# One more pair of K tiles by seven products in the first feed-forward of an encoder block

## The chip, the cores and the metric

The kernel runs on one core of a Trainium2 chip. The metric is the time of one execution in microseconds (us), device time, median of the runs. The whole block runs as one program; nothing is computed on the host but the arrangement of weights and inputs in memory.

## What is computed

One layer of an encoder on 256 tokens of width 2048: a feed-forward at half weight, a mixing stage with two recurrent branches, a cross-attention to 256 memory tokens, a second feed-forward, a last norm. The change lies in the first feed-forward alone:

```python
def rms_norm(x, g):
    y = x * rsqrt(mean(x * x, axis=-1, keepdims=True) + EPS)
    return y * g

def swiglu(h, w_up, w_down):                       # w_up 2048 x 11264, w_down 5632 x 2048
    gate, up = split(h @ w_up, 2, axis=-1)
    return (silu(gate) * up) @ w_down

x = x + 0.5 * swiglu(rms_norm(x, ffn1_norm), ffn1_w_up, ffn1_w_down)
...                                                # mixing, cross-attention
x = x + 0.5 * swiglu(rms_norm(x, ffn2_norm), ffn2_w_up, ffn2_w_down)
```

All inputs and weights are fp32.

## The kernel before

**Precision.** Matmuls run on the type fp32r. Each operand is split in a high part (a copy on ScalarE into fp32r, L138) and a low part (raw less high, on VectorE, L139), both by the helper `split`. A product a b is then three matmuls: high by high, low by high and high by low (function `three`: L547, L548 and, later, L550).

**Tiling of the first feed-forward.** The 5632 hidden features go in eleven groups of 512, numbered 0 to 10. In a group the 2048 input features are eight pairs of K tiles of 128, here called p0 to p7 (the digit is the pair's index, not its place in the order). The weights of a pair and a group are one tile `raw` of 128x2048, 1 MB: four blocks of 512 columns, up and gate for each of the two K tiles. x is the stationary side, 128x128, and there are two token tiles; so a pair is a 2x2 by 2x2 block product: token tiles by K tiles by (up, gate).

- A *plain* pair does it with eight products of 128x128 by 128x512, 24 matmuls. A *mixed* pair also has eight, written so that its results fall into the accumulators of the seven-product scheme; it needs differences of x ("less") as well. Both split the raw tile as a whole.
- A *fast* pair does it with seven products, 21 matmuls. It needs sums of the weights' blocks, four blocks `td`, made on VectorE (L285, L287, L288: `td` or, elsewhere, a raw buffer), and sums of x. It splits three raw blocks (128x1536, giving h and l) and the four blocks of sums in two halves of 128x1024 (giving th and tl). The halves of th are called th1 and th2 here.
- A fast pair that *adds* (p3, p4, p5, p6 from group 4 on) makes l of the raw blocks without VectorE: ScalarE writes the negated high part (L293), and a transfer from GpSimd's queue adds the raw weights to it in memory (L294).

**Down products.** A group's hidden features are multiplied by w_down in tiles of 128x2048 too, four such tiles after each group from group 3 on, called d1 to d4 here; one of four is made with the adding transfer (L254, L255, L263), the others are plain (split as a whole). The hidden features are turned by TensorE (L588) in between.

**Order.** `ffn_order` writes the order of pairs and down tiles by hand. `weights` prepares two tiles ahead of the one in use (three where a tile's low part is added by transfer). Within that, a scheduler in the layer below fixes the order of instructions of every engine when the program is built; at run time each engine works its queue in that order. Buffers are rings: raw 3, h 3 (h and th of a pair take two), l 3, wide 3 (td, tl and the evicted accumulators), slots 22 (operands of x, hidden operands, workspace). A load on SyncE's queue goes when its ring's buffer is free.

**Before the change**, from group 4 on the order is p1, p3, p4, p0, p2, p5, p6, p7, and p0 is mixed, the others fast. In group 3, p0 and p6 are mixed and made with the adding transfer.

**Sums of x.** `operand_pairs` makes for each pair of K tiles the split operand, the differences (`less`) and, in its inner function `sums`, the sums. For even pairs the differences would lie in the place of the sums, so the pairs in `BOTH` keep them in a tile of their own, `xd`, and get sums as well; these are made later, at places 16, 17 and 26 of the plan (`late_sums`).

Of the kernel before, what the change touches and what calls it, by code (L numbers as in the profile page):

```python
# [8 lines left out]
F32 = mybir.dt.float32  # L9
F32R = mybir.dt.float32r  # L10
ACT = mybir.ActivationFunctionType
ALU = mybir.AluOpType

P = 128
# [24 lines left out]
PAD = 16  # L39


def ffn_order(every=False):

    out = [(("mixed" if p > 5 else "fast") if every else "plain", 0, p) for p in range(8)]
    down = [("down", 0, 1, c, 0) for c in range(4)]  # L50
    for g in range(1, NG):
        if every:
            out += [("fast", g, p) for p in (1, 3, 4, 0, 2, 5, 6, 7)]
        elif g < 3:
            out += [(("mixed", "fast")[p % 2], g, p) for p in (0, 1, 2, 3, 5, 4, 7, 6)]
        else:
            out += [("mixed" if p == 0 or g == 3 and p == 6 else "fast", g, p)
                    for p in ((1, 3, 0, 4, 2, 6, 5, 7) if g == 3 else (1, 3, 4, 0, 2, 5, 6, 7))]
        if g > 2 and g % 2:
            down = [("down", g - 2, 2, c, b) for c in range(4) for b in (g - 2, g - 1)]  # L60
        n = 2 if g < 3 else 4
        out, down = out + down[:n], down[n:]
    return out + [("down", NG - 2, 2, c, b) for c in range(4) for b in (NG - 2, NG - 1)]


def adds(name, e):

    return name == "ffn1" and e[0] == "fast" and e[1] > 3 and e[2] in (3, 4, 5, 6)


def sums_ready(name, e):

    made = () if e[1] < 3 else (0, 5, 7) if e[1] % 2 else (0, 3, 5, 7)
    return name == "ffn2" and e[0] == "fast" and e[2] not in made
# [3 lines left out]
def block_kernel(ctx: ExitStack, tc: tile.TileContext, xT, xin, memT, vec, gfin, bgate, lruw, wu1, wd1, win, wv,  # L78
                 wg, wab, wout, wq, wk, wvm, wo, wu2, wd2, out_):
    nc = tc.nc  # L80
    pe, dve, act, sp = nc.tensor, nc.vector, nc.scalar, nc.sync
# [23 lines left out]
    def slot(dt=F32, name="slot"):  # L105
        return slots.tile([P, 1024], dt, name=name, tag="slot")
# [24 lines left out]
    x = [xt[k // 4][:, (k % 4) * T:(k % 4 + 1) * T] for k in range(KT)]  # L131
    ident = col("ident", 0, P)

    done = {}


    def split(h, l, raw):
        done["high"] = act.activation(h, raw, ACT.Copy).ins  # L138
        done["low"] = dve.tensor_tensor(out=l, in0=raw, in1=h.bitcast(F32), op=ALU.subtract).ins  # L139
# [4 lines left out]

    plan, ahead, made_ahead = [], [], []
    orders = {"ffn1": ffn_order(), "ffn2": ffn_order(every=True)}

    def plan_ffn(name, wu, wd):
        for e in orders[name]:
            src = wd[e[4], e[3]] if e[0] == "down" else wu[e[1], e[2]]  # L150
            kind = "fast" if e[0] == "fast" else "added" if e[:2] == ("mixed", 3) else "plain"
            if e[0] == "down" and 0 < e[4] < NG - 1 and e[4] % 2 == 0 and e[3] % 2:
                kind = "added"
            if adds(name, e):
                kind = "fast added"
            if sums_ready(name, e):
                kind = "ready"
                t = kept.tile([P, 2048], F32, name=f"t{e[1]}_{e[2]}")
                made_ahead.append((src, t))
                src = src, t  # L160
            plan.append(((name,) + e, src, kind))
# [4 lines left out]
    def plan_rows(name, w, g):  # L166
        plan.extend(((name, g, kq), w[g, kq], "plain") for kq in range(w.shape[1]))

    plan_ffn("ffn1", wu1, wd1)
    first_middle = len(plan)  # L170
    for hf in range(2):
# [12 lines left out]
    for name, w in (("mv", wvm), ("o", wo)):  # L184
        for g in range(4):
            plan_rows(name, w, g)
    first_second = len(plan)
    plan_ffn("ffn2", wu2, wd2)

    head, rest = [], {}  # L190
# [297 lines left out]

    BOTH = [2, 4, 6]
    xd = []

    def operand_pairs(src, gain, q, xg, out, every=False):


        for a in src:
# [8 lines left out]
            if every:  # L506
                less = None
                if q == 3:
                    if not i:
                        xd.append(slot(F32R, "xd"))  # L510
                    less = [xd[-1][:, a:a + 256] for a in (512 * i, 512 * i + 256)]
            elif 2 * q + i in BOTH:
                n = 512 * (BOTH.index(2 * q + i) % 2)
                if not n:
# [4 lines left out]
        def sums(which=((0, "less"), (0, "sums"), (1, "less"), (1, "sums"))):  # L519
            s = slot(name="xs")  # L520
            for i, ((h, l), less) in enumerate(out):
                a = [xg[:, i * 512 + j * P:][:, :P] for j in range(4)]

                def made(h, l, n, at, terms):
                    o = [s[:, at + j * P:][:, :P] for j in range(n)]
                    for j, (x, y, op) in enumerate(terms(o)):
                        dve.tensor_tensor(out=o[j], in0=x, in1=y, op=op)
                    split(h, l, s[:, at:at + n * P])

                if less and (i, "less") in which:  # L530
                    made(*less, 2, 0, lambda o: ((a[0], a[1], ALU.subtract), (a[2], a[3], ALU.subtract)))
                if (every or i or 2 * q in BOTH) and (i, "sums") in which:
                    if not every and not i and len(which) > 1:
# [31 lines left out]
    def ffn(name, pairs, sq, then, begin=(), sums=()):  # L565
# [38 lines left out]
        for at, e in enumerate(order):  # L604
# [3 lines left out]
            if kind != "down":  # L608
# [3 lines left out]
                for i, (a, b, n) in enumerate(PRODUCTS["ready" if sums_ready(name, e) else kind]):  # L612
                    u = uses[g, n]
                    if u[0] == (p, i):
                        accs[n] = bank()
                    own, less = pairs[p]
                    products.append((accs[n], part(own, a, P) if a >= 0 else part(less, -1 - a, P), part(w[b // 4] if fast else w, b % 4, 512),
                                     u[0] == (p, i), u[-1] == (p, i)))
                three(products, 3 if adds(name, e) else 0, adds(name, e) and p == 6)
                last = at + 1 == len(order) or order[at + 1][1] != g or following == "down"  # L620
                ends = kind != "plain" and uses[g, 0][-1][0] == p
# [51 lines left out]
    pairs1, sq1 = [], TokenSquares()  # L673
# [30 lines left out]
    def late_sums(q):  # L704
        with tc.issue_after(done["low"]):
            sums1[q](((0, "sums"),))

    for q, i in ((1, 16), (2, 17), (3, 26)):
        rest[i] = lambda q=q: late_sums(q)


    par = const.tile([P, 96], F32, name="par")
# [56 lines left out]
    xs = xs2.tiles  # L769
# [372 lines left out]
    for g in range(4):  # L1142
# [4 lines left out]
        for t in range(2):  # L1147
            s = slot(F32R, "vs")
            f = scoped["tmp2"].tile([P, 512], F32, name="vf", tag="part")
# [7 lines left out]
    for h in range(HEADS):  # L1157
        for j in range(4):
            acc = bank()
            for t in range(2):  # L1160
                ps = probs[h][:, t * 512:(t + 1) * 512]
                s = vs[h, t]
# [153 lines left out]
```

## Time and profile before

| what | us |
|---|---|
| median of 3 runs | 2426.14 |
| lowest and highest | 2425.5 and 2426.68 |
| span of the profiled execution | 2425.5 |
| first feed-forward in it, to the turn of the last group's hidden features | 648.0 |
| one of the groups 4 to 9 in it | 61.7 to 61.8 |
| group 10, between the same marks | 63.6 |

How it is read: the profile names engines PE (TensorE matmuls), PEld (its weight loads), DVE (VectorE), ACT (ScalarE), POOL (GpSimd), SP (SyncE); a letter q marks an engine's queue issuing a transfer. An instruction is named by its line in the kernel, then output <- inputs. In a row of the timeline the first number is the start in us from the start of the span, the second the time to the end of the last of xN merged instructions, and brackets give the idle time of the engine before it and what ended it. Matmuls overlap in their records, so their spacing is read from starts. The clock granted to TensorE is 0.998 of full speed over the span, so it plays no part. The lines themselves are shown in the prediction.

### The profile page before, as it was taken

How to read it: one execution, taken by the hardware profiler on the slowest of the kernel's cores; microseconds unless marked ns; L12 is line 12 of the kernel's file. 1: busy time of each engine (PE TensorE's matmuls, PEld its weight loads, DVE VectorE, ACT ScalarE, POOL GpSimd, SP SyncE). 2: the span in 40 equal slices, each digit the busy share in tenths (PEclk: the TensorE clock that was granted, in tenths of full speed). 3: DMA queues.
4: the chain of work that ended last, by engine and by line, in shares of the span. 5: the costliest groups of instructions: out<-in, count | busy, mean ns of one | idle time of the engine just before them, and what ended most of it. 6: DMA issues, size and time to landing. Idle time of an engine off the chain costs nothing.

```text
span 2425.5 us, 30763 instructions
## 1 busy us (share of the span) xinstructions
PE 2409.3 (99%) x12139; PEld 2013.6 (83%) x12139; DVE 2025.6 (84%) x2260; ACT 1455.0 (60%) x1485; POOL 102.2 (4%) x166
## 2 busy tenths in 40 slices
PE   9999999999999999999999999999999999999998
PEld 8888888888788888888888888888888788888887
DVE  7999999998876868779776788777789999999995
ACT  8567677777664454476434555445676666666664
POOL 0000000000000000000000000000000000000000
PEclk9999999999999999999999999999999999999999
DMA  7579999988858776778989889977798878787873
GB/s 294 195 229 287 272 272 270 275 269 268 266 183 323 268 289 241 294 289 323 346 313 349 310 332 354 335 272 263 264 343 308 285 266 293 273 286 276 294 273 144
DMA packets 102385, 684.31 MB, mean 282 GB/s; under 512 B 11361, under 2 KB 11617, under 8 KB 29281
## 3 DMA queue, kind: packets, MB, share of 16 engines
q1 hardware_dynamic: 78192, 518.68, 57.5%
q0 software_dynamic: 23328, 162.54, 22.4%
q8 instruction: 95, 1.56, 0.2%
q10 hardware_dynamic: 720, 1.13, 0.1%
q14 instruction: 50, 0.40, 0.0%
HBM read 619.39 MB, written 62.91 MB: 281 GB/s over the span
## 4 chain that ended last, share of the span: by engine, by line
PE 91%; DVE 3%; DMA 3%; ACT 1%; issue 1%; ACTq 0%; DVEq 0%; SPq 0%
PE acc L547 16%; PE acc L548 16%; PE acc L550 16%; PE acc L313 11%; PE acc L338 8%; PE acc L341 8%; PE acc L339 8%; PE acc L316 6%; DMA raw<-wd 2%; DVE tl L139 1%; ACT h L138 1%; DVE l L139 1%; PE acc L588 1%; PE acc L477 1%; DMA t<-prep 0%
## 5 line engine op out<-in xcount | busy, mean ns | idle before, releaser
L138 ACT ACTIVATE h<-raw 128x2048 fp32r<-128x2048 f32 (+3 forms) x578 | 870.5, 1531 | 620.2 <-PE acc L339 189.6
L139 DVE TENSOR_TENSOR l<-raw,h 128x2048 fp32r<-128x2048 f32 (+2 forms) x406 | 837.3, 2065 | 187.6 <-ACT h L138 186.1
L547 PE MATMUL acc<-h,xh 128*128 128x512 f32 x1241 | 485.2, 392 | 2.7 <-ACT h L138 2.4
L548 PE MATMUL acc<-h,xl 128*128 128x512 f32 x1241 | 483.0, 390 | 0.0
L338 PE MATMUL acc<-h,ops 128*128 128x512 f32 x832 | 326.8, 393 | 0.0
L339 PE MATMUL acc<-h,ops 128*128 128x512 f32 x832 | 324.5, 390 | 0.0
L547 PEld LDWEIGHTS acc<-h,xh 128*128 128x128 f32 x1241 | 233.3, 188 | 56.2 <-ACT h L138 8.0
L547 PE MATMUL acc<-h,hidop 128*128 128x512 f32 x704 | 276.5, 393 | 2.3 <-ACT h L138 2.2
L313 PE MATMUL acc<-ops,h 128*128 128x512 f32 x1152 | 278.2, 393 | 0.0
L548 PE MATMUL acc<-h,hidop 128*128 128x512 f32 x704 | 274.8, 390 | 0.0
L548 PEld LDWEIGHTS acc<-h,xl 128*128 128x128 f32 x1241 | 233.3, 188 | 47.5
L313 PEld LDWEIGHTS acc<-ops,h 128*128 128x128 f32 x1152 | 211.7, 188 | 41.6
L139 DVE TENSOR_TENSOR tl<-raw,h 128x1024 fp32r<-128x1024 f32 x172 | 203.7, 1220 | 14.9 <-ACT h L138 14.5
L341 PE MATMUL acc<-l,ops 128*128 128x512 f32 x832 | 205.8, 389 | 0.0
L550 PE MATMUL acc<-l,hidop 128*128 128x512 f32 x704 | 189.3, 389 | 0.0
L138 ACT ACTIVATE h<-td 128x1024 fp32r<-128x1024 f32 x126 | 131.3, 1057 | 92.9 <-PE acc L548 42.3
L341 PEld LDWEIGHTS acc<-l,ops 128*128 128x128 f32 x832 | 156.2, 188 | 32.4
L338 PEld LDWEIGHTS acc<-h,ops 128*128 128x128 f32 x832 | 156.2, 188 | 32.2
L339 PEld LDWEIGHTS acc<-h,ops 128*128 128x128 f32 x832 | 156.3, 188 | 31.5
L139 DVE TENSOR_TENSOR tl<-td,h 128x1024 fp32r<-128x1024 f32 x126 | 152.0, 1220 | 31.2 <-ACT h L138 31.0
L200 DVE TENSOR_TENSOR prep<-prep 128x512 f32<-128x512 f32 x232 | 159.7, 689 | 20.9 <-DMA prep<-wu 17.1
L550 PE MATMUL acc<-l,xh 128*128 128x512 f32 x645 | 176.4, 389 | 0.0
(242 smaller groups left out, 2739.4 us busy)
## 6 DMA issues: line engine op xcount, KB each, us to landing
raw<-wu SPq DMA_DIRECT2D x114, 1024.0 KB, 6.3
raw<-wd SPq DMA_DIRECT2D x88, 1024.0 KB, 6.3
prep<-wu POOLq DMA_DIRECT2D x58, 1024.0 KB, 7.8
t<-prep POOLq DMA_DIRECT2D x58, 1024.0 KB, 7.8
raw<-t SPq DMA_DIRECT2D x58, 1024.0 KB, 6.9
raw<-wu SPq DMA_DIRECT2D x58, 768.0 KB, 5.0
raw<-win SPq DMA_DIRECT2D x40, 1024.0 KB, 4.8
raw<-wg SPq DMA_DIRECT2D x32, 1024.0 KB, 6.1
```

The costliest lines, as they stand in the source:

```text
L138: done["high"] = act.activation(h, raw, ACT.Copy).ins
L139: done["low"] = dve.tensor_tensor(out=l, in0=raw, in1=h.bitcast(F32), op=ALU.subtract).ins
L200: dve.tensor_tensor(out=b[o], in0=b[x], in1=b[y], op=ALU.subtract)
L313: pe.matmul(acc, h[:, k * P:(k + 1) * P], xs[k], start=k == 0, stop=False)
L316: done["product"] = pe.matmul(acc[:, :T], l[:, k * P:(k + 1) * P], xs[k][:, :T], start=False, stop=k == KT - 1).ins
L338: pe.matmul(accs[t], x[:, t * P:][:, :P], h[j], start=first and j == 0, stop=False)
L339: pe.matmul(accs[t], x[:, T + t * P:][:, :P], h[j], start=False, stop=False)
L341: done["product"] = pe.matmul(accs[t], x[:, t * P:][:, :P], l[j], start=False, stop=last and j == 3).ins
L477: pe.transpose(acc[:, z * T + t * P:][:, :P], tile[:, t * 512 + (2 * y + z) * P:][:, :P], ident)
L547: pe.matmul(acc, ah, bh, start=start, stop=False)
L548: pe.matmul(acc, al, bh, start=False, stop=False)
L550: pe.matmul(acc, ah, bl, start=False, stop=stop)
```

## The change

From group 4 on, p0 is a fast pair too, and it is third in the order instead of fourth: p1, p3, p0, p4, p2, p5, p6, p7. The pairs that add stay the same four. p0 is added to `BOTH`, so its differences, which the mixed product of the groups 1 to 3 reads, go to `xd`, and its sums take the place after the first 512 columns. These sums are made by a new function `first_sums` at place 33 of the plan, which is in group 3, from the high and low parts of x added together. The orders of the groups 0 to 3 are only written in another way (the table `FIRST`: p plain, m mixed, M mixed with the adding transfer, f fast, a fast with the adding transfer).

```diff
+FIRST = [
+    "p0 p1 p2 p3 p4 p5 p6 p7",
+    "m0 f1 m2 f3 f5 m4 f7 m6",
+    "m0 f1 m2 f3 f5 m4 f7 m6",
+    "f1 f3 M0 f4 f2 M6 f5 f7",
+    "f1 a3 f0 a4 f2 a5 a6 f7",
...
+]
+KINDS = {"p": "plain", "m": "mixed", "M": "mixed", "f": "fast", "a": "fast"}
+
+def first(g):
+    return [(KINDS[e[0]], g, int(e[1])) for e in FIRST[g].split()]
 
 def ffn_order(every=False):
-    out = [(("mixed" if p > 5 else "fast") if every else "plain", 0, p) for p in range(8)]
+    out = [("mixed" if p > 5 else "fast", 0, p) for p in range(8)] if every else first(0)
...
-        elif g < 3:
-            out += [(("mixed", "fast")[p % 2], g, p) for p in (0, 1, 2, 3, 5, 4, 7, 6)]
         else:
-            out += [("mixed" if p == 0 or g == 3 and p == 6 else "fast", g, p)
-                    for p in ((1, 3, 0, 4, 2, 6, 5, 7) if g == 3 else (1, 3, 4, 0, 2, 5, 6, 7))]
+            out += first(g)
...
-    return name == "ffn1" and e[0] == "fast" and e[1] > 3 and e[2] in (3, 4, 5, 6)
+    return name == "ffn1" and e[0] == "fast" and f"a{e[2]}" in FIRST[e[1]]
...
-    BOTH = [2, 4, 6]
+    BOTH = [0, 2, 4, 6]
...
+    def first_sums():
+        (h, l), _ = pairs1[0]
+        s = slot(name="xs")
+        a, o = ([s[:, n + j * P:][:, :P] for j in range(4)] for n in (0, 512))
+        with tc.issue_after(done["low"]):
+            dve.tensor_tensor(out=s[:, :512], in0=h[:, :512].bitcast(F32), in1=l[:, :512].bitcast(F32), op=ALU.add)
+            for j, (x, y, op) in enumerate(((a[1], a[3], ALU.add), (o[0], a[0], ALU.subtract),
+                                            (a[1], a[0], ALU.subtract), (a[2], o[1], ALU.subtract))):
+                dve.tensor_tensor(out=o[j], in0=x, in1=y, op=op)
+            split(h[:, 512:], l[:, 512:], s[:, 512:])
+
+    rest[33] = first_sums
```

In the built program the order of SyncE's and GpSimd's transfers is unchanged but for the order of p0's and p4's tiles; on TensorE, VectorE and ScalarE the order changes from group 3 to the end of the first feed-forward and nowhere after it.

More of the change, by code (lines that the diff above doesn't have):

```diff
@@ L150, in plan_ffn @@
             src = wd[e[4], e[3]] if e[0] == "down" else wu[e[1], e[2]]
-            kind = "fast" if e[0] == "fast" else "added" if e[:2] == ("mixed", 3) else "plain"
+            kind = "fast" if e[0] == "fast" else "added" if name == "ffn1" and e[0] == "mixed" and f"M{e[2]}" in FIRST[e[1]] else "plain"
             if e[0] == "down" and 0 < e[4] < NG - 1 and e[4] % 2 == 0 and e[3] % 2:
```

6 rows, old and new, of the table FIRST are left out of this document.

## The prediction

> **What bounds the kernel now.** I read the page first, then windows of the first feed-forward group by group, then the order of work on each engine inside one group.
>
> ```profile
> PE 2409.3 (99%) x12139; PEld 2013.6 (83%) x12139; DVE 2025.6 (84%) x2260; ACT 1455.0 (60%) x1485; POOL 102.2 (4%) x166
> ```
>
> TensorE is busy 99% of the span, which says "TensorE bound" as a mean. The change touches seven groups, 4 to 10 of the eleven numbered 0 to 10, so these are read by themselves. The windows below run from one set of L588 transposes to the next; columns are length, busy time of PE, PEld, DVE, ACT and POOL, granted clock, DMA share, GB/s.
>
> ```profile
> 275.50:337.30 61.80, 61.66 (x276) 50.84 (x275) 56.41 (x57) 44.05 (x37) 4.35 (x5) 1.00 0.91 272
> 337.30:399.10 61.80, 61.76 (x277) 50.91 (x276) 56.36 (x57) 44.30 (x37) 4.35 (x5) 1.00 0.90 272
> 584.40:648.00 63.60, 61.94 (x276) 50.74 (x275) 55.84 (x55) 44.23 (x37) 4.37 (x5) 1.00 0.87 263
> ```
>
> A group lasts 61.8 us and TensorE has next to no gap in it, but VectorE is busy 56.4 of these (91%) and the DMA engines 90%. So three resources are close together, and what the first sheds matters only as far as the other two follow. Two windows inside a group, a pair by seven products and the pair by eight:
>
> ```profile
> 343.64:348.40 4.76, 4.76 (x22) 3.94 (x21) 2.98 (x5) 4.76 (x5) 0.88 (x1) 1.00 0.91 213
> 357.92:363.36 5.44, 5.44 (x25) 4.51 (x24) 5.44 (x6) 4.05 (x3) 0.87 (x1) 1.00 0.83 283
> ```
>
> Both are gapless: 21 matmuls in 4.76 us, 0.2267 us each, and 24 in 5.44.
>
> Where a group is tightest shows at its last pair, p7. First ScalarE there, then TensorE:
>
> ```profile
> 376.30 1.92 ACT L138 ACTIVATE h<-raw 128x2048 fp32r<-128x2048 f32 x1 [0.62 <-PE acc L548]
> 378.54 1.06 ACT L138 ACTIVATE h<-td 128x1024 fp32r<-128x1024 f32 x1 [0.32 <-DVE td L288]
> 379.51 1.90 ACT L138 ACTIVATE h<-raw 128x2048 fp32r<-128x2048 f32 x1
> ...
> 379.23 0.39 PE L550 MATMUL acc<-l,xh 128*128 128x512 f32 x1
> 379.66 0.49 PE L547 MATMUL acc<-h,xh 128*128 128x512 f32 x1
> ```
>
> The three ScalarE rows are the high part of the first down tile (d1), of p7's second half of weight sums (I call it th2 of p7), and of the second down tile (d2). TensorE's next matmul starts at 379.66, just after th2 ends at 379.60 and 0.43 after the one before: some 0.2 us lost per group. So th2 of p7 is already the last thing to arrive. In group 10 it is later, because d1, ahead of it in ScalarE's queue, waits for its transfer:
>
> ```profile
> 625.62 1.92 ACT L138 ACTIVATE h<-raw 128x2048 fp32r<-128x2048 f32 x1 [2.25 <-DMA raw<-wd]
> 627.44 1.04 ACT L138 ACTIVATE h<-td 128x1024 fp32r<-128x1024 f32 x1
> ...
> 628.53 0.50 PE L547 MATMUL acc<-h,xh 128*128 128x512 f32 x1 [1.66 <-ACT h L138]
> ```
>
> TensorE stands 1.66 us there. The pattern to keep in mind: a down tile's transfer, a split on ScalarE that waits for it, th2 behind that split, TensorE behind th2.
>
> **The change, part by part.** *Products.* Seven groups lose one product, three matmuls: 5.44 - 4.76 = 0.68 us each, 4.76 us in all, or 0.20% of the span. That is the whole direct gain and, at 0.2%, about what a measurement of this kernel can tell from no change.
>
> *Weight work of p0.* It was one split (ScalarE 128x2048, VectorE 128x2048). It becomes three sums, a split of 128x1536 and two of 128x1024. VectorE's prices in group 6:
>
> ```profile
> L139 DVE TENSOR_TENSOR tl<-td,h 128x1024 fp32r<-128x1024 f32 x14 | 16.8, 1221 | 4.9 <-ACT h L138 4.9
> L139 DVE TENSOR_TENSOR l<-raw,h 128x2048 fp32r<-128x2048 f32 x4 | 9.1, 2285 | 0.0
> L285 DVE TENSOR_TENSOR td<-raw 128x1024 f32<-128x1024 f32 x7 | 8.5, 1219 | 0.0
> L139 DVE TENSOR_TENSOR l<-raw,h 128x1536 fp32r<-128x1536 f32 x3 | 5.3, 1754 | 0.0
> L288 DVE TENSOR_TENSOR td<-raw,td 128x512 f32<-128x512 f32 x7 | 4.8, 691 | 0.1
> L287 DVE TENSOR_TENSOR td<-raw,td 128x512 f32<-128x512 f32 x7 | 4.8, 689 | 0.1
> ```
>
> By durations that is 1.22 + 0.69 + 0.69 + 1.75 + 2 x 1.22 - 2.29 = 4.5 us more per group. Instructions that do not read the one before start about 0.085 us before its recorded end (below: 355.10 + 2.29 = 357.39, the next at 357.31), and five instructions are added, so I take 4.5 - 0.4 = 4.1. VectorE then works about 60.5 us in a group that TensorE could do in 61.1. [...]
>
> *Where the 4.1 us go.* VectorE from the second pair to the end of the pairs (group 6), only the rows used:
>
> ```profile
> 346.83 2.36 DVE L139 TENSOR_TENSOR tl<-td,h 128x1024 fp32r<-128x1024 f32 x2 [1.75 <-ACT h L138]
> ...
> 355.10 2.29 DVE L139 TENSOR_TENSOR l<-raw,h 128x2048 fp32r<-128x2048 f32 x1
> 357.31 0.69 DVE L287 TENSOR_TENSOR td<-raw,td 128x512 f32<-128x512 f32 x1
> ...
> 366.06 2.36 DVE L139 TENSOR_TENSOR tl<-td,h 128x1024 fp32r<-128x1024 f32 x2 [1.06 <-ACT h L138]
> ...
> 368.34 1.22 DVE L285 TENSOR_TENSOR td<-raw 128x1024 f32<-128x1024 f32 x1
> 369.59 0.69 DVE L287 TENSOR_TENSOR td<-raw,td 128x512 f32<-128x512 f32 x1
> 370.32 0.69 DVE L288 TENSOR_TENSOR td<-raw,td 128x512 f32<-128x512 f32 x1
> ...
> 377.82 0.69 DVE L288 TENSOR_TENSOR td<-raw,td 128x512 f32<-128x512 f32 x1
> ```
>
> The last row, which ends at 378.51, is what th2 of p7 waits for now. Between 346.83 and that end there is one gap, 1.06 us; ahead of it one of 1.75, which ends when ScalarE has p3's th:
>
> ```profile
> 344.39 1.47 ACT L293 ACTIVATE l<-raw 128x1536 fp32r<-128x1536 f32 x1
> 345.76 1.99 ACT L138 ACTIVATE h<-td 128x1024 fp32r<-128x1024 f32 x2
> ```
>
> The first row is the negated copy for the next accumulating pair, p4. That pair now comes one later, and in the changed program the copy comes after this th. The buffer of th is free when p1 has used its first six matmuls, at 343.64 + 1.36 = 345.0, so th starts some 0.65 earlier (345.1 for 345.76), and VectorE's chain with it. The row at 370.32 is the last reader of p6's raw tile; the raw ring has three buffers, so its end, 371.01, lets d2's transfer go:
>
> ```profile
> 371.07 0.33 SPq L270 DMA_DIRECT2D raw<-wd  x1
> ...
> raw<-wd SPq DMA_DIRECT2D x1, 1024.0 KB, 7.6
> ```
>
> After the change that reader stands behind 4.1 us more work and behind one more 1.1 us split (p6's first half, by the new order of VectorE's queue), less 0.65 for the earlier start, 0.6 for some five dependent pairs that the new order interleaves (L287 starts 1.25 after the L285 that it reads, 0.12 later than a free one would by 1.22 - 0.085), and 1.06 if the gap closes: 371.07 + 4.1 + 1.1 - 0.65 - 0.6 - 1.06 = 374.0; 375.0 if the gap stays. Landing 7.6 later: 381.6.
>
> *The order on ScalarE.* In the built changed program all seven groups have d1's and d2's high parts both ahead of th2 of p7; before, d2's came after it. So th2 waits for d2's transfer. Queued behind that waiting split are th2 and the group's first eviction (L634); behind th2 stand VectorE's last split of p7 and TensorE. 381.6 + 1.90 (row at 379.51) + 1.04 (row at 627.44) = 384.55. TensorE's order is changed too: p7's last four th2 matmuls now follow eight matmuls of d1 and are the 171st to 174th of the group, so TensorE without a wait gets there at 343.64 + 170 x 0.2267 = 382.2. It waits 2.35 us. With the shortest and longest landing of such a load,
>
> ```profile
> raw<-wu SPq DMA_DIRECT2D x1, 1024.0 KB, 4.8
> ...
> raw<-wd SPq DMA_DIRECT2D x1, 1024.0 KB, 11.8
> ```
>
> the wait is 0 (378.8, ScalarE is then free in time) or 384.55 + 4.2 = 388.75, so 6.5 us. I take 2.35: the 7.6 row is this very transfer, under the same load of accumulating transfers.
>
> Per group: +2.35, -0.68, and the old 0.2 at the same place falls into the new wait: +1.47. Times seven: +10.3. The down part of a group stays TensorE's: of the 4.9 us that VectorE waited for th in a group (the first row of its prices), 1.75 and 1.06 lie in the pairs, so 2.1 in the down part, which take up what VectorE comes later.
>
> *ScalarE's own load* grows by one split of 1536 (between 1.06 for 1024 and 1.92 for 2048, about 1.5) and two of 1024 less one of 2048, 1.7 us per group, to 46 of 61.8: nothing by itself. Loads and accumulating transfers keep number, size and order on SP's and POOL's queues; only their moments shift.
>
> *Sums of x made late*, once, in group 3: one 128x512 sum from high and low part, four 128x128, one split, at these prices:
>
> ```profile
> L139 DVE TENSOR_TENSOR xl<-xs,xh 128x512 fp32r<-128x512 f32 x1 | 0.7, 689 | 0.0
> L527 DVE TENSOR_TENSOR xs<-xg 128x128 f32<-128x128 f32 x2 | 0.6, 286 | 0.0
> ```
>
> 0.69 + 4 x 0.29 + 0.69 = 2.5 us of VectorE. What covers it in group 3 is one gap, and the time in which th2 of p7 waits for d1's transfer anyway:
>
> ```profile
> 241.94 1.23 DVE L139 TENSOR_TENSOR tl<-td,h 128x1024 fp32r<-128x1024 f32 x1 [0.91 <-ACT h L138]
> ...
> 253.10 1.92 ACT L138 ACTIVATE h<-raw 128x2048 fp32r<-128x2048 f32 x1 [1.55 <-DMA raw<-wd]
> ```
>
> About 1.5 us of cover, so +1.0; bounds 0 and 2.5. The pair's differences move from xh and xl to the xd tile: same instructions, nothing.
>
> **Sum.** The profiled execution spans 2425.5, which is the lowest of the three runs; their median is 0.6 higher. -4.76 - 7 x 0.2 + 7 x 2.35 + 1.0 = +11.3: 2436.8 against 2425.5, so 2437 on the median's scale.
>
> **Rivals.** *Faster.* Place: d2's landing. If it lands before 379.3 (382.2 less 1.90 and 1.04), that is within 5.3 us of its issue at 374.0, th2 is in time and all 4.76 us and the old 1.4 arrive, less up to 1.0 in group 3: about 2421. For it: 4.8 is seen, and TensorE's new order gives th2 eight matmuls of cover. Against: the 4.8 row is p6's load, issued with no accumulating transfer near it. Chance 0.13.
>
> *No change.* A smaller wait, about 1 us per group, takes the product back: p2's th2 stands on ScalarE behind p6's negated copy, which waits for p6's load; or p5's accumulated low part, issued as late as before but used two pairs' time earlier. 7 x (1.0 - 0.88) + 1.0 = +2: 2428. For it: p4's and p0's work moves p6's load and p5's copy about as much as d2's load, a few us, and I estimate margins of about 1 us from the same rows. Against: a wait there does not add to the one at p7 but comes ahead of it, and leaves that one in place. Chance 0.24.
>
> *VectorE bound throughout.* It keeps the 5.4 us of idle that it has in a group now, less the 1.06: 60.5 + 4.3 = 64.8 us a group, 3.0 more, +21 +1: 2448. For it: every pair then hands over with no slack. Against: most of that idle is in the down part, which can shrink. Chance 0.08.
>
> The forecast has 0.55; its own range is 2430 to 2446, by a landing a little over 1 us to either side. The range over all, 2423 to 2448, leaves out most of the faster case and the tail above. Faster by over 0.2% (4.9 us): 0.13; within: 0.24; slower: 0.63.
>
> **What would show it.** Right: groups of about 63.3 us in place of 61.8; ScalarE's d2 split (the 128x2048 one before th2 of p7) idle before it, ended by a transfer from wd; TensorE idle in the middle of p7 and d1, ended by ScalarE; VectorE over 95% busy in a group. Wrong: groups of 61 us with no such idle time (the faster case), TensorE waiting first in p2 or p5, or group 3 longer by more than 2.5 us.

## The result: slower by half a per cent

The changed kernel takes 2439.28 us (median of five runs, 2435.89 to 2440.49) against 2426.14 for the kernel before on the same chip (median of five, 2424.71 to 2427.44). The ratio is 1.0053 with a 95% interval of 1.0042 to 1.0064, so +12.9 us (10 to 15.5). The forecast was 2437, with a range of 2423 to 2448.

The profiled execution of the changed kernel is the lowest of its five runs: span 2434.1, time 2435.89. In the trace the seven changed groups account for +11.0 us (434.8 us before, 445.8 after, from the first transposes at 213 us to the last at 648.0 and 658.8); the groups 0 to 3 are unchanged, and the rest of the program, which the change doesn't touch, is 2.2 us shorter. So the two profiled executions differ by 8.6 us, some 4 less than the medians; where the slower executions of the changed kernel lose more, no trace here shows. I read the groups.

First the line of the engines on the page after; then windows of the changed kernel from one set of transposes to the next (groups 5, 6 and 10; columns as in the prediction):

```profile
PE 2410.9 (99%) x12118; PEld 2005.6 (82%) x12118; DVE 2054.1 (84%) x2301; ACT 1465.0 (60%) x1500; POOL 102.2 (4%) x166
```

```profile
276.20:339.60 63.40, 62.02 (x273) 50.01 (x272) 60.35 (x63) 45.57 (x39) 4.34 (x5) 1.00 0.90 266
339.60:404.80 65.20, 62.42 (x274) 49.77 (x273) 60.53 (x63) 45.33 (x39) 4.35 (x5) 1.00 0.87 259
595.70:658.80 63.10, 61.99 (x274) 49.90 (x273) 59.26 (x61) 45.16 (x38) 4.37 (x5) 1.00 0.90 266
```

The mean of the page (TensorE 99% busy) has not moved, and says nothing of this change. The groups do: group 5 from 61.8 to 63.4, group 6 from 61.8 to 65.2, with three matmuls less in each and 3.9 and 4.2 us more of VectorE (56.41 to 60.35, 56.36 to 60.53).

The chain of waits shows what changed hands. Group 5, before and then after:

```profile
by line: PE acc L550 28.6%; PE acc L547 27.2%; PE acc L548 26.8%; DVE tl L139 3.9%; ACT h L138 3.5%; DVE l L139 2.7%; issue 2.2%; DVE td L285 1.8%; PE acc L588 1.4%; DVE td L288 1.1%; DVE td L287 1.0%; DVEq L139 0.1%; ACTq L138 0.0%
```

```profile
by line: DMA raw<-wu 31.1%; DVE tl L156 14.8%; issue 11.8%; DMA raw<-wd 11.3%; ACT h L155 10.5%; DVE td L302 7.3%; ACT l L310 4.7%; DVE l L156 4.3%; DVE td L305 3.4%; ACT h L280 2.9%; DVE td L304 2.1%; DVE x L679 1.9%; ACT hidop L609 1.5%; 
```

Before, the group was for the most part a chain of matmuls. After, no matmul is in it: it goes from a load of weights (31.1% and 11.3%) through VectorE and ScalarE to the next load. The group now runs at the pace of the ring of raw tiles: load, splits and sums, buffer free, next load. (In groups 7 and 9 there is no matmul in the chain either; in the others of the seven 3 to 25% of it are matmuls.)

**The forecast wait is there.** Group 5 at p7, ScalarE and then TensorE (the three ScalarE rows are d1's split, d2's split, th2 of p7):

```profile
318.27 1.92 ACT L155 ACTIVATE h<-raw 128x2048 fp32r<-128x2048 f32 x1 [2.36 <-DMA raw<-wd]
320.70 1.92 ACT L155 ACTIVATE h<-raw 128x2048 fp32r<-128x2048 f32 x1 [0.50 <-DMA raw<-wd]
322.52 1.04 ACT L155 ACTIVATE h<-td 128x1024 fp32r<-128x1024 f32 x1
...
323.61 0.50 PE L564 MATMUL acc<-h,xh 128*128 128x512 f32 x1 [1.22 <-ACT h L155]
```

**But not in every group.** In group 7 the same pattern sits a few pairs earlier. Two negated copies (L310) wait for their loads, the th behind them is late, TensorE waits for it:

```profile
428.70 1.49 ACT L310 ACTIVATE l<-raw 128x1536 fp32r<-128x1536 f32 x1 [0.73 <-DMA raw<-wu]
430.09 1.04 ACT L155 ACTIVATE h<-td 128x1024 fp32r<-128x1024 f32 x1
431.04 1.47 ACT L312 ACTIVATE h<-raw 128x1536 fp32r<-128x1536 f32 x1
433.43 1.49 ACT L310 ACTIVATE l<-raw 128x1536 fp32r<-128x1536 f32 x1 [0.92 <-DMA raw<-wu]
434.83 1.99 ACT L155 ACTIVATE h<-td 128x1024 fp32r<-128x1024 f32 x2
...
435.92 0.50 PE L564 MATMUL acc<-h,xh 128*128 128x512 f32 x1 [0.88 <-ACT h L155]
```

To size both, I add up for each group the distance between the starts of successive 128x512 matmuls beyond 0.227 us. This is TensorE's lost time, in us, for groups 4 to 10:

| | 4 | 5 | 6 | 7 | 8 | 9 | 10 | sum |
|---|---|---|---|---|---|---|---|---|
| after, where p7 meets d1 | 1.7 | 1.5 | 0.1 | 0.4 | 0.4 | 0.2 | 1.3 | 5.5 |
| after, elsewhere in the pairs | 0.7 | 1.1 | 4.3 | 2.4 | 2.6 | 2.3 | 1.0 | 14.4 |
| before, both | 0.9 | 0.5 | 0.4 | 0.4 | 0.4 | 0.4 | 2.2 | 5.2 |

19.9 less 5.2 is 14.7 us lost; less 4.76 for the products that are gone, +9.9 of the +11.0 that the groups grew.

### The profile page after: what moved, and what is told of

Read it like the earlier page. It is cut to its first block, busy times and chain, and to the rows that moved or that the text cites. A ratio compares the mean times of both kernels' runs of the same rounds, so it can differ in the third digit from the quotient of the medians.

```text
span 2434.1 us, 30812 instructions
## 1 busy us (share of the span) xinstructions
PE 2410.9 (99%) x12118; PEld 2005.6 (82%) x12118; DVE 2054.1 (84%) x2301; ACT 1465.0 (60%) x1500; POOL 102.2 (4%) x166
## 4 chain that ended last, share of the span: by engine, by line
PE 79%; DVE 9%; DMA 5%; ACT 4%; issue 3%; ACTq 0%; DVEq 0%; SPq 0%
PE acc L564 12%; PE acc L565 12%; PE acc L567 12%; PE acc L330 11%; PE acc L355 8%; PE acc L358 8%; PE acc L356 8%; PE acc L333 6%; DVE tl L156 3%; DMA raw<-wu 3%; ACT h L155 3%; DMA raw<-wd 2%; DVE l L156 2%; DVE td L302 2%; DVE td L305 1%
## 5 line engine op out<-in xcount | busy, mean ns | idle before, releaser
L565 PE MATMUL acc<-h,xl 128*128 128x512 f32 x1228 | 476.3, 390 | 0.0
L155 ACT ACTIVATE h<-td 128x1024 fp32r<-128x1024 f32 x140 | 146.0, 1053 | 81.6 <-DVE td L302 33.5
L156 DVE TENSOR_TENSOR tl<-td,h 128x1024 fp32r<-128x1024 f32 x140 | 170.4, 1218 | 11.9 <-ACT h L155 10.9
L567 PE MATMUL acc<-tl,xh 128*128 128x512 f32 x624 | 177.8, 391 | 1.1 <-DVE tl L156 0.9
```

The source lines that it names most:

```text
L565: pe.matmul(acc, al, bh, start=False, stop=False)
L567: pe.matmul(acc, ah, bl, start=False, stop=stop)
```

## The experiments

Theory 1 is the prediction's: ScalarE works a fixed queue in which splits that wait for late loads stand ahead of splits that TensorE needs now. Theory 2: VectorE's 4.1 us more work per group is the bound. Theory 3, taken up for the second set: the place of p0 in the order costs, not its kind. Ratios are to the kernel before, run beside each on the same chip, with 95% intervals; "us" after a ratio is the ratio times 2426.1. In the expectations, p2, p7 and so on are pairs as in the prediction.

**1. d2's split behind th2 of p7.** One instruction on ScalarE moved, VectorE's order unchanged:

```diff
+            with tc.issue_after(highs[-2]) if second else nullcontext():   # second: the tile is d2
                 ahead.append((k, prepare(src, kind, 4 if i < 4 else 1)))
```

> The changed kernel with one difference: on ScalarE the second down tile's split of groups 4 to 10 is queued behind th2 of p7, as before the change; VectorE's order is the same. Theory 1 (splits on ScalarE that wait for late transfers hold up the splits behind them): the waits at that place, 4.6 us in the seven groups of the changed kernel's profile, go: 2434.5 to 2436.5. Theory 2 (VectorE's added work is the bound, whatever ScalarE's order): 2438 to 2440, the waits turn up elsewhere.

1.0028 [1.0017, 1.0038], 2432.9 us: about half of the loss is gone, 6 of 13 us (2 to 10 with both intervals). That is a little under theory 1's range and well under theory 2's. ScalarE in group 5 now has d1's split, an eviction, th2, and only then d2's split:

```profile
316.72 1.92 ACT L155 ACTIVATE h<-raw 128x2048 fp32r<-128x2048 f32 x1 [1.57 <-DMA raw<-wd]
318.78 0.60 ACT L656 ACTIVATE ev<-acc 128x512 f32<-128x512 f32 x1
319.27 1.05 ACT L155 ACTIVATE h<-td 128x1024 fp32r<-128x1024 f32 x1
320.22 1.92 ACT L155 ACTIVATE h<-raw 128x2048 fp32r<-128x2048 f32 x1
```

TensorE's loss at p7 falls from 5.5 to 1.0 us over the seven groups; elsewhere it stays (14.4 to 13.6).

**2. The negated copies behind the waited-for th as well.**

```diff
+            with tc.issue_after(highs[-4]):
                 act.activation(l[:, 512:], raw[:, 512:], ACT.Copy, scale=-1.0)
```

> As the run before, and the negated copy of an accumulating pair is also queued behind th2 of the pair two places ahead (p6's copy behind th2 of p2). Theory 1: the waits for th2 of p2 (0.4 to 1.3 us in five groups) go too: 2430 to 2434. Theory 2: 2437 to 2440.

On ScalarE of the built program only p6's copy moves against run 1: the half of p2's sums that stood behind it now stands ahead of it. 1.0019 [1.0009, 1.0028], 2430.7 us; the loss elsewhere falls from 13.6 to 8.4 us, while 1.7 of it come back at p7. With run 1 this shows that the order on ScalarE was about 8 of the 13 us (5 to 12 with both intervals); the step from run 1 to this one lies within their intervals. Theory 1's range (2430 to 2434) holds it, theory 2's (2437 to 2440) does not. What holds the other part it doesn't settle.

**3. The product alone.** The kernel before, the last of p0's eight products left out in groups 4 to 10 (part of the sum is missing), weights and order as before:

```diff
+                if name == "ffn1" and g > 3 and p == 0:
+                    products.pop()
```

> The kernel before, with p0 still mixed, but the last of its eight products left out in groups 4 to 10: 21 matmuls less and nothing else (part of the sum over p0 is missing). Both theories: the direct gain alone, 4.8 us and up to 1.4 us of the old wait: 2420 to 2422. If VectorE or the transfers are already as tight as TensorE, less: 2423 to 2426.

0.9975 [0.9965, 0.9985], -6.1 us, as both theories had it. Group 6:

```profile
335.64:396.86 61.22, 61.07 (x274) 50.30 (x273) 56.43 (x57) 44.01 (x37) 4.36 (x5) 1.00 0.92 276
```

61.2 us with the old weight work. TensorE's saving is real, 0.6 us of a group and about 2.5 in group 10, whose old wait went too; the change spends it, and 13 us more, on the weights.

**4. No sums of p0's weights.** The changed kernel without the three VectorE sums; the splits of th and tl read the raw tile (part of the computation is left out).

```diff
+                td = raw if bare else scoped["wide"].tile([P, 2048], F32, name="td", tag="wide")
...
+            if not bare:
                 dve.tensor_tensor(out=two[0], ...)      # and the two other sums
```

> The changed kernel without the three VectorE instructions that make the sums of p0's weights in groups 4 to 10 (its th and tl are split from the raw tile instead): 2.4 us of VectorE less per group, the rest stays. Theory 2: most of the loss goes, 2420 to 2425. Theory 1: the transfers start earlier by the same 2 us, but the order on ScalarE may keep some of the wait: 2425 to 2431.

1.0028 [1.0016, 1.0039], 2432.9 us: above what either theory gave. VectorE fell from 60.1 to 58.2 us a group, the groups by 0.2 us in the mean (445.8 to 444.1 in the profiled runs), and the loss at p7 rose from 5.5 to 9.3 us while it fell elsewhere from 14.4 to 9.3. In these two executions what is gained in the pairs is given back behind d2. The ratios say more, 6 us: the changed kernel's profiled execution is its fastest, this one's among the slower of its runs. The run has two flaws. p0's raw tile is held longer, until its last split; in 12 it is not. And the scheduler, given less VectorE work, built another order on ScalarE too, with p6's copy behind a half of p2's sums, which is the move of run 2. So the gain is not VectorE's alone.

**5. The same, with both reorders of 2.**

> The changed kernel without the three VectorE sums of p0's weights (the second half of the weights is split from the raw tile; leaves out part of the computation), and with d2's split and the negated copies queued on ScalarE behind the halves of weight sums that TensorE needs first: the run without the sums and the run with both reorders in one. Theory 1: the waits of 1.3 to 1.7 us behind d2, seen in six of seven groups of the run without the sums, go: 2433.5 - 8 = 2425.5, at best 2420 if the other order's waits go with them; ratio 0.9975 to 1.0000. Theory 2 alone: VectorE at 58 us of 62 was no bound any more in the run without sums, so the order brings little: 2431 to 2434. If both prices add without sharing, 2431.7 (both reorders) - 5.8 (the difference the sums made) = 2426.

1.0008 [0.9998, 1.0017], 2428.1 us, no longer told from the kernel before, and between the theories (2420 to 2425.5 and 2431 to 2434); the loss at p7 falls from 9.3 to 1.3 us. 1.0053 less what runs 2 and 4 each took would be 0.9994, but both contain the move of p6's copy, so it is counted twice there. Run 2 has almost this order on ScalarE and all of VectorE's work: 1.0019 against 1.0008 is 2.7 us, with an interval of some 3 us to either side. What the three sums cost by themselves is thus not told from nothing.

**6 to 8. Place and kind apart.** Three kernels which, with the changed one, make a square: p0 by eight or by seven products, in the old fourth or the new third place, all with the late sums of x.

```diff
-    "f1 a3 f0 a4 f2 a5 a6 f7",      # the changed kernel: seven products, third
+    "f1 a3 a4 m0 f2 a5 a6 f7",      # 6: eight, fourth (the late sums alone)
+    "f1 a3 m0 a4 f2 a5 a6 f7",      # 7: eight, third
+    "f1 a3 a4 f0 f2 a5 a6 f7",      # 8: seven, fourth
```

> The changed kernel with the old order of pairs (p1 p3 p4 p0 ...) and p0 by eight products in groups 4 to 10; only the sums of x made late in group 3 are left of the change. Theory 1 (ScalarE's strict order and late transfers are the price): the late sums cost nothing in group 3, which measured 52.2 us before and after, so 2426 to 2427, ratio 1.000 to 1.0005. Theory 2 (VectorE's added work is the price): the same, since the seven groups have the old work. My prediction's own term was +1.0 us, 2427. If the late sums cost up to their 2.5 us of VectorE, 2428.5.

> The changed kernel with p0 third in the order of groups 4 to 10 but still by eight products: the place alone. In the built program d2's split on ScalarE stands behind th2 of p7, as before the change, and VectorE has its old work. Theory 1 and theory 2: within 2 us of the kernel with the late sums alone, 2425 to 2429, no wait of TensorE at p7 above 0.3 us. Theory 3 (the place is what costs: p4's accumulated copy and p5's come one pair later, their consumers no later): most of the loss is here, 2432 to 2440, with TensorE waiting in p4 or p5.

> The changed kernel with p0 by seven products but in its old fourth place: the kind alone. Theory 1: in the built program d1 and d2 both stand ahead of th2 of p7 as in the changed kernel, so the wait there stays, 2434 to 2441. Theory 2: VectorE has the same added work, so the same 2434 to 2441. Theory 3 (the place costs): the product's gain comes through, 2421 to 2426.

| | fourth | third |
|---|---|---|
| eight products | 1.0006 [0.9997, 1.0016] | 1.0091 [1.0072, 1.0110] |
| seven products | 1.0201 [1.0184, 1.0218] | 1.0053 [1.0042, 1.0064] |

This I had not expected. The place alone costs 22 us, the kind alone 49, and both together 13: each of the two edits is worse without the other. All three theories missed runs 7 and 8. In run 7 VectorE has nearly its old work (56.8 us) and d2's split stands behind th2, and it is slow; in run 8 both are as in the changed kernel, and it is far slower.

Run 7, group 6, ScalarE (d1's split, th2 of p7) and TensorE, and the landing of p5's and p6's loads:

```profile
381.62 1.91 ACT L155 ACTIVATE h<-raw 128x2048 fp32r<-128x2048 f32 x1 [1.31 <-DMA raw<-wd]
383.44 1.04 ACT L155 ACTIVATE h<-td 128x1024 fp32r<-128x1024 f32 x1
...
384.53 0.50 PE L564 MATMUL acc<-h,xh 128*128 128x512 f32 x1 [1.94 <-ACT h L155]
```

```profile
raw<-wu SPq DMA_DIRECT2D x2, 1024.0 KB, 8.7
```

It is the same pattern with d1 in d2's part, and TensorE has no matmuls of d1 ahead of th2 here that could cover it. Why is d1's load late? With p0 third, p4's accumulating transfer starts 13.5 us after the group's start instead of 9.0, just ahead of p5's load (14.8); p5's and p6's loads land after 8.1 and 9.3 us where they took 6.4 and 4.8 before, p5's tile comes free later, and d1, which takes its buffer, is issued at 30.5 instead of 27.8. In groups 6 and 10 a second loss follows the wait: the granted clock is half for 3.4 us, and some eight matmuls start 0.43 us apart, 1.6 us lost in each.

Run 8, group 5: ScalarE ahead of p5's negated copy (the last row, p5's and p6's), TensorE, and the accumulating transfer that p5's copy starts:

```profile
300.79 1.49 ACT L155 ACTIVATE h<-raw 128x1536 fp32r<-128x1536 f32 x1 [1.09 <-DMA raw<-wu]
302.56 1.06 ACT L155 ACTIVATE h<-td 128x1024 fp32r<-128x1024 f32 x1 [0.28 <-DVE td L305]
304.92 1.06 ACT L155 ACTIVATE h<-td 128x1024 fp32r<-128x1024 f32 x1 [1.29 <-DVE td L302]
306.02 1.49 ACT L312 ACTIVATE h<-raw 128x1536 fp32r<-128x1536 f32 x1
307.41 2.85 ACT L310 ACTIVATE l<-raw 128x1536 fp32r<-128x1536 f32 x2
...
320.20 1.22 PE L567 MATMUL acc<-l,xh 128*128 128x512 f32 x2 [5.43 <-DMA l<-wu]
...
322.50 0.63 PE L564 MATMUL acc<-h,xh 128*128 128x512 f32 x1
322.92 0.63 PE L565 MATMUL acc<-h,xl 128*128 128x512 f32 x1
```

```profile
l<-wu POOLq DMA_DIRECT2D x1, 768.0 KB, 10.9
```

p5's raw tile was there at 302.94, but in this program's order its copy stands behind p2's split, a half of p0's sums, a half of p2's and p5's own high part: it starts 4.5 us later, the transfer lands 10.9 us after its issue, and TensorE stands 5.43 us. In all seven groups this wait costs 4.4 to 5.6 us of the 7 to 10 that TensorE loses there. In the kernel before and in the changed one only one half of sums stands between p2's split and the copy. So the third place keeps p5's copy early: the two edits belong together, by the order of one queue. This is read from the traces; no run moved the copy alone.

After the wait TensorE is slow as well. The last two TensorE rows start 0.42 us apart instead of 0.227, and the window of group 5 has a granted clock of 0.95 (1.00 in the changed kernel's windows):

```profile
281.12:350.37 69.25, 63.42 (x274) 51.20 (x273) 60.26 (x63) 45.42 (x39) 4.34 (x5) 0.95 0.81 244
```

In each of the seven groups the clock is half for 3.4 or 6.8 us from about this wait on, and seven to twelve matmuls start at that distance: some 12 of the 49 us, beside 33 for the waits.

**9. Run 7 without p4's accumulating transfer**, its low part made on VectorE instead:

```diff
-    "f1 a3 m0 a4 f2 a5 a6 f7",
+    "f1 a3 m0 f4 f2 a5 a6 f7",
```

> The run with p0 third by eight products (2447.6, ratio 1.0091), but p4's low part made on VectorE, so that its accumulating transfer is gone in groups 4 to 10; nothing else is moved. VectorE gets 1.75 us more per group, 56.9 to 58.6. Theory 1 (place: p4's accumulating transfer, one pair later, runs beside p5's load, which lands late, and d1's load after it): the wait of 1.9 to 2.5 us at p7 goes, 7 x 2 = 14 us less, 2430 to 2434, and d1's load is issued some 2 us earlier in its group. Theory 2 (VectorE's work): it gets slower, 2448 to 2458.

1.0014 [1.0005, 1.0023], 2429.5 us: 19 us back, although VectorE works more (58.0 for 56.8). TensorE at the same place of group 6, and the loads of p5 and p6:

```profile
381.24 0.50 PE L564 MATMUL acc<-h,xh 128*128 128x512 f32 x1 [0.30 <-ACT h L155]
```

```profile
raw<-wu SPq DMA_DIRECT2D x2, 1024.0 KB, 4.7
```

4.7 us for 8.7, and d1 at 29.0. Theory 2 had this run slower than run 7. That p4's accumulating transfer in its later place is most of the price of the place is shown; that it acts through p5's load is read from these rows.

**10. No load for p0.** The changed kernel, p0 computed from p3's raw tile (its own weights are left out), all engines' queues unchanged.

```diff
+        raw = last[-1] if again else raw_tile()
...
+            if not again:
                 sp.dma_start(raw, src)
```

> The changed kernel without p0's load in groups 4 to 10 (p0 is computed from p3's raw tile, so its own weights are left out); every engine's instructions and their order stay. One of thirteen loads of a group is gone. Theory 1 (late loads hold up ScalarE's strict order): the loads behind it land earlier, the waits of 1 to 2 us at p7 and p2 shrink to a few tenths, groups of 61.5 to 62.3 us, 2425 to 2431. Theory 2 (VectorE's 60.3 us of work): nothing is taken from VectorE, groups stay at 63 to 64 us, 2436 to 2441.

1.0057 [1.0042, 1.0072]: no gain. (A group has twelve loads and five accumulating transfers, not thirteen loads as I wrote.) Group 6:

```profile
340.50:405.20 64.70, 62.38 (x274) 49.83 (x273) 60.50 (x63) 45.30 (x39) 4.34 (x5) 1.00 0.82 240
```

The DMA engines went from 0.87 to 0.82 busy and the group from 65.2 to 64.7 only. Theory 1 as I had put it for this run, that the loads are late because there are many of them, is wrong; theory 2's range, 2436 to 2441, holds the result. They are late because they are issued late: p5's at 17.2, p7's at 29.2, d1's at 32.8 us after the group's start, as with p0's load in (17.5, 29.5, 33.1). A load went when its buffer was free: in group 6 of the changed kernel p0's last sum ends at 357.01, and p5's load goes at 357.08. The run leaves that as it was: p5's load takes the buffer that p0 reads, with or without a load of p0's own, and goes after p0's last sum on VectorE. So it tests the number of loads and not what frees the buffers.

**11. The kernel before with d1's split behind th2 of p7**, a version meant to beat it:

```diff
+            with tc.issue_after(done["high"]) if first else nullcontext():   # first: the tile is d1
                 ahead.append((k, prepare(src, kind, 4 if i < 4 else 1)))
```

> The kernel before, with d1's split on ScalarE queued behind th2 of p7 in groups 4 to 10 (d2's stands there already). Theory 1: TensorE's wait behind d1's transfer in group 10 (1.66 us and what the stall of PE's clockwork adds, 1.8 lost in all) and 0.5 in group 4 go, the other groups stay at 61.8: 2.0 to 2.4 us less, ratio 0.9990 to 0.9992. Theory 2: nothing moves, ratio 1.0000. If the wait in group 10 only passes to d1's own matmuls, 0.5 us less.

1.0031 [1.0020, 1.0043], slower, which neither theory had. In the kernel before the wait of group 10 costs 1.82 us by the starts of the matmuls, 1.66 of it idle. Groups 4 and 10 do what was expected (62.3 to 61.8 and 63.6 to 61.9), but group 6 goes from 61.8 to 67.1 and group 8 to 63.7. Group 6: TensorE's wait, the VectorE row that holds it up (p2's first sum waits for p2's load, and the tl that TensorE needs stands behind it), then p2's load (SyncE) and p4's accumulating transfer (GpSimd), and their landing:

```profile
359.31 0.74 PE L553 MATMUL acc<-tl,xh 128*128 128x512 f32 x2 [3.44 <-DVE tl L139]
...
356.90 1.23 DVE L288 TENSOR_TENSOR td<-raw 128x1024 f32<-128x1024 f32 x1 [5.05 <-DMA raw<-wu]
...
345.22 0.33 SPq L282 DMA_DIRECT2D raw<-wu  x1
345.19 0.88 POOL L297 DMA_DIRECT2D l<-wu  x1 [4.34 <-ACT l L296]
```

```profile
raw<-wu SPq DMA_DIRECT2D x1, 1024.0 KB, 11.6
l<-wu POOLq DMA_DIRECT2D x1, 768.0 KB, 12.7
```

and the same two in the kernel before:

```profile
344.55 0.33 SPq L279 DMA_DIRECT2D raw<-wu  x1
346.26 0.88 POOL L294 DMA_DIRECT2D l<-wu  x1 [4.00 <-ACT l L293]
```

```profile
raw<-wu SPq DMA_DIRECT2D x1, 1024.0 KB, 7.9
l<-wu POOLq DMA_DIRECT2D x1, 768.0 KB, 9.1
```

1.7 us apart they take 7.9 and 9.1 us; 0.03 us apart 11.6 and 12.7. That they start together does not explain it: in group 7 of this same run they start 0.07 us apart and take 7.9 and 10.5. And the edit did more than it says. In every group from 5 on the built program also has p3's negated copy ahead of a half of p1's sums, where it waits for its load, and another order on VectorE; p2's load went when p3's last sum ended there, at 345.16. So the run doesn't price d1's split alone, and which of these differences costs the 5 us of group 6 is not shown. 1.6 of them are matmuls at half the clock after the wait.

**12. Less VectorE work, p0's raw tile freed as before.** The changed kernel without the two VectorE splits that make p0's tl:

```diff
+        if high_only:
+            for a in (0, 1024):
+                done["high"] = act.activation(th[:, a:a + 1024], td[:, a:a + 1024], ACT.Copy).ins
+            return (h, l), (th, th)
```

> The changed kernel without the two VectorE splits that make the low part of p0's weight sums in groups 4 to 10 (TensorE multiplies the high part in their place, which leaves out part of the computation). VectorE is spared 2 x 1.22 = 2.4 of the 4.1 us added per group; the three sums, p0's other splits, all loads and TensorE's work stay, and p0's raw tile has the same readers. My prediction's chain (VectorE's work puts off the last reader of p6's raw tile, that puts off d2's load, d2's split holds th2): d2's load is issued about 2.4 us earlier in its group (38.8 to 36.4 after the group's start), groups of 61.8 to 62.5 us, 2426 to 2431. Rival (the order of the accumulated copies on ScalarE and the accumulating transfer beside p5's load set the moments, VectorE follows): d1's and d2's loads stay at about 32 and 38 us after the group's start, groups of 63 to 64 us, 2435 to 2440. VectorE as the bound throughout: 2.4 us off every group, 2439 - 17 = 2422.

1.0031 [1.0019, 1.0042], 2433.7 us: between the two. Group 7, its window, then d1's split, d2's split, th2 and TensorE:

```profile
403.10:466.10 63.00, 61.53 (x274) 50.12 (x273) 58.14 (x61) 45.66 (x39) 4.36 (x5) 1.00 0.89 262
```

```profile
444.63 1.92 ACT L155 ACTIVATE h<-raw 128x2048 fp32r<-128x2048 f32 x1 [2.51 <-DMA raw<-wd]
446.91 1.92 ACT L155 ACTIVATE h<-raw 128x2048 fp32r<-128x2048 f32 x1 [0.36 <-DMA raw<-wd]
448.73 1.04 ACT L155 ACTIVATE h<-td 128x1024 fp32r<-128x1024 f32 x1
...
449.82 0.50 PE L568 MATMUL acc<-h,xh 128*128 128x512 f32 x1 [1.06 <-ACT h L155]
```

In group 6 d2's load moves from 38.8 to 36.4 us after the group's start, the 2.4 us taken from VectorE, one for one (in groups 5, 7 and 8 by 0.5 to 2.0). The waits in the pairs halve (14.4 to 7.1), and the wait at p7 takes over, 1.0 to 2.0 us in six of seven groups (8.6 in all): the wait that the prediction describes, now the larger part. Of 17 us of VectorE's work 5 come back (1 to 9 with both intervals).

But here too the scheduler moved p6's copy, and these 5 us contain that move. In group 7 of the changed kernel (above) the copy at 433.43 directly follows p5's high part (L312), and th comes after it; here a th stands ahead of the copy:

```profile
428.78 1.47 ACT L312 ACTIVATE h<-raw 128x1536 fp32r<-128x1536 f32 x1
430.16 1.04 ACT L155 ACTIVATE h<-td 128x1024 fp32r<-128x1024 f32 x1
431.10 1.48 ACT L310 ACTIVATE l<-raw 128x1536 fp32r<-128x1536 f32 x1
```

Of the 7.3 us by which the waits in the pairs fall, 3.2 lie in p2, where the move took as much in run 2, and 3.7 in p4, where TensorE had waited for VectorE. So the work on VectorE has a price, but no run here gives it by itself.

## Why the prediction was right, and where it was not

**The product** was priced at 0.68 us a group; run 3 shows 0.6. None of it arrived, as forecast.

**VectorE, +4.1 us a group.** The windows say +3.9 and +4.2 in groups 5 and 6, which makes VectorE 95% and 93% busy; the sign that I gave was over 95%. By the durations of the rows alone the step was 4.5; their starts, 0.085 us closer where an instruction does not read the one before, made it 4.1, which is nearer to what the windows show.

**d2's load.** Forecast to go 36.7 us after the start of group 6 and to land after 7.6; it went at 38.8 and landed after 6.8, so at 45.6 instead of 44.3. Before, in order of time, d1's load, then after, d1's and d2's:

```profile
365.06 0.33 SPq L270 DMA_DIRECT2D raw<-wd  x1
```

```profile
372.70 0.33 SPq L287 DMA_DIRECT2D raw<-wd  x1
378.44 0.33 SPq L287 DMA_DIRECT2D raw<-wd  x1
```

```profile
raw<-wd SPq DMA_DIRECT2D x1, 1024.0 KB, 6.8
```

Here the step failed in part. I followed one buffer, d2's, and left all loads ahead of it where they had been. But p5's, p6's, p7's and d1's tiles come from the same ring: d1's load moved as well, from 27.8 to 33.1 us after the group's start, and ahead of it p5's from 14.5 to 17.5, p6's from 20.1 to 23.2 and p7's from 23.0 to 29.5. p0's weights sit early in the ring, and these loads behind them slipped by 3 to 6.5 us.

**TensorE's wait at p7**, forecast 2.35 us in each of seven groups: 16.5 in all, measured 5.5. Its mechanism is shown (1 removes it by moving d2's split), its size was not. The other 14.4 us are lost earlier in the group: about 4.5 where p7's own split waits for p7's load, 3.7 in p4, whose sums come late from VectorE, 3.4 in p2, whose half of sums stands behind p6's negated copy, and 2.0 in p0. The wait in p2 is the one that the rival "no change" named; the largest, behind p7's load, was in none of my cases. In the rival I argued that a wait in the pairs "comes ahead of" the one at p7 "and leaves that one in place". It does not: in groups 6 to 9 the pairs take the loss (2.3 to 4.3 us, with 0.1 to 0.4 at p7), in 4, 5 and 10 p7 does (1.3 to 1.7, with 0.7 to 1.1 in the pairs). The total, +11.0 in the groups against a sum of +11.3, fits better than its parts did, and that is partly luck.

**Sums of x**, +1.0: measured 0.0. Group 3, in which they run, is 52.2 us before and after, and run 6 shows 1.0006 [0.9997, 1.0016]. The two rows that I took as their cover (241.94 and 253.10) are of group 4, not group 3, a misreading; the table ahead of the prediction has the like slip, group 4 lasted 62.3 us.

**The base.** I took the span of 2425.5 for the time of the lowest run. An execution takes 1.8 us more than its span (2435.89 against 2434.1), so the profiled execution of before took about 2427.3.

**VectorE bound throughout** (2448) did not come true: 9 gives VectorE more work and is faster, and of what 12 takes from it at most about half comes back. **The faster case** needed d2 to land within 5.3 us of an issue at 374.0; it was issued at 378.44.

What stays open: even with both reorders and without the sums (5) the kernel is 8 us above run 3, where TensorE has the same work. TensorE still loses 12 us there in the seven groups, in waits of up to 1.2 us at two or three places of a group; I did not try to remove them one by one. VectorE's own share of the 13 us stays open too, since no run takes work from it at an unchanged order on ScalarE (4, 5 and 12 come nearest).

None of the runs that do the whole computation beats the kernel before.

## What to carry to other kernels

When a step is made longer on an engine that prepares data, don't follow its one next buffer: here the loads that take a tile from the same ring slipped too (p5's to d2's, by 3 to 6.5 us in group 6), and of the 19.9 us lost 14.4 appeared ahead of the place that I had followed, so price the ring for the total and don't count on the place. Splits that waited for their loads made the one behind them late (in group 5 ScalarE sat idle 2.36 us ahead of d1's and 0.50 ahead of d2's, th2 stood behind them, and TensorE waited 1.22 us); look in the built order, for each engine, at what stands behind each load-dependent instruction, since moving one split decided some 6 us here, and by the traces the place of p5's copy most of 49. Look there after every edit, also on the engines that it doesn't name: leaving out VectorE work moved a copy on ScalarE (4, 12), and moving one split moved another copy (11), so that these runs did not test one thing. And where a gain per group is as small as 0.68 us, two edits can't be judged one at a time: place alone cost 22 us, kind alone 49, both 13.

## What the runs showed of the hardware

A load of 1 MB took 4.7 us with no accumulating transfer near (run 9). With an accumulating transfer started less than 2 us from it, it took 4.8 to 11.9 us in groups 4 to 10 of the kernel before and of the changed one. When the nearest one started does not say how long: 7.9 us with one 1.7 us behind it, 11.6 with one 0.03 us ahead of it in group 6 of run 11, 7.9 with one 0.07 us behind it in group 7 of that run, and 6.9 in the kernel before (the load at 360.33) with one 0.04 us ahead. The accumulating transfers of 768 KB took 9.1, 12.7, 10.5 and 10.5 us. What makes the difference stays open. Taking one load in twelve away left d1's landing in group 6 at 10.3 us (10.0 with it).

The granted clock of TensorE went to half after some of the longer waits, for 3.4 or 6.8 us (over the span it was 0.991 in run 8, 0.997 in run 7 and 0.999 in the changed kernel): after those of 4.2 to 5.4 us in all seven groups of run 8 and the 3.44 us of run 11. The length of the wait alone does not decide it: in run 7 it followed the waits of groups 6 (1.94 us) and 10 (2.49 us), and not those of groups 5 (1.94 us) and 7 (2.49 us). In the kernel before and in the changed one the groups kept 1.00.

The shortest accumulating transfer of 768 KB in groups 5 to 8 of the kernel before and of the changed one took 6.8 us (the changed kernel, issued at 301.13). What two transfers at the same time cost each other no run here settles.
